# A shorter planned cost per VectorE and ScalarE operation in the scheduler of a hybrid attention and RG-LRU block

## The chip, the cores and the metric

The kernel runs on one core of one Trainium2 chip. The metric is the device time of one launch in microseconds. The version before takes 910.19 us (median of three runs, 908.47 to 910.79). Its profiled execution took 907.51 us, of which the profile's span covers 905.8 us; the remaining 1.7 us lie around the span.

TensorE is called PE in the rows, VectorE DVE, ScalarE ACT, GpSimd POOL, and the queue that issues most of the transfers SP. PEld is the loading of TensorE's stationary operand.

## The reference

One layer of a decoder block on 1024 tokens of width 1024, in float32:

```
h      = rmsnorm(x, norm_g) * (1 + scale) + shift          # scale, shift, gate from c @ w_ada
q, k, v, g_attn, xr, g_rnn, m_attn, m_rnn = split(h @ w_in)
y_attn = window_attention(rope(q), rope(k), v, sinks) * silu(g_attn)    # window 128, 16 heads, 4 kv heads
xr     = causal_depthwise_conv(xr, conv_w, conv_b)          # width 4
y_rnn  = rg_lru(xr, rg_wa, rg_wx, ...) * silu(g_rnn)        # a scan along the tokens
merged = sigmoid(m_attn) * (y_attn @ w_attn_proj) + sigmoid(m_rnn) * (y_rnn @ w_rnn_proj)
out    = rmsnorm(x + gate * (merged @ w_out), final_g)
```

The gates of the RG-LRU are products with four blocks of 256 x 256; its recurrence is `h[t] = a[t] h[t-1] + b[t]`.

## The kernel before

**Numbers.** A float32 operand is used as two float32r parts, a high one (a rounded copy, made by ScalarE) and a low one (the rest, made by VectorE); a product is the sum of high x high, high x low and low x high.

**Stages.** (1) Normalisation, transposition of x and four first column blocks. (2) The block products: the columns of `w_in`, two blocks of 128 at a time. Each such `Pair` is a 2 x 2 block product done with seven half products in Winograd's form. (3) Attention, 32 units `u` of one kv head and 128 queries each; between two units stand the last products of stage 2 and the products with `w_rnn_proj` (tile `rp`). (4) The products with `w_attn_proj`, the output projection `out`, the last norm.

**Slots.** Stage 2 and the start of stage 3 are laid out in slots. One slot holds one half product of 12 matmuls (`product`, line 711), and `SLOT` = 2.75 is what the planner thinks it takes; a gate product of the RG-LRU puts 24 matmuls (tile `pgate`, line 1027, `GATE` = 5.5) ahead of a slot's product. A pair starts every seven slots. What a pair needs at fixed slots (`at_slot`): loads of weights six to four slots ahead (tile `r`), sums of weight halves on VectorE (tile `ws`, line 733), the high parts on ScalarE two slots ahead (tile `wh`, line 106 or 108), the low parts on VectorE one slot ahead (tile `wl`, line 112 or 114), and the evacuation of PSUM banks (`keep`, `join`, the sinks).

**Background.** All else that VectorE and ScalarE do in stage 2 stands in three lists and is put between the fixed steps by `background(d)`, once per slot: `waiting[0]` (the RG-LRU after its gates: sigmoids, tanh, exp, square root, scan, `after_gates`), `waiting[1]` (the causal convolution, gate weights, the values `v` of attention) and `idle` (the gate vector and the seven combinations of `w_out`, `w_out_gate` and `w_out_blocks`; their sources are loaded into tile `wr`, their results stored to `wo_d`). Every step is a tuple of a letter, a cost on ScalarE, a cost on VectorE and a function. The planner keeps three clocks: `Load.pe`, the planned start of the slot on TensorE, and `Load.act` and `Load.dve`, when the two engines will be through with what was given to them. A group from the `waiting` lists is put when its planned end lies at most 2.8 (or 2.2) behind the slot's end, a group from `idle` when it lies at most `SLACK` behind it. No clock of the chip is read: the result is a fixed order of instructions on each engine.

The costs are written in the steps: 0.69 for a VectorE operation on 128 x 512, 0.62 for a ScalarE copy of that size, 1.22 to 1.28 for VectorE on 128 x 1024, 2.29 for the scan. The lines that spend them:

```
    def put(st_):
        Load.act = max(Load.act, Load.pe) + st_[1]
        Load.dve = max(Load.dve, Load.pe) + st_[2]
        st_[3]()
```

**Start of stage 3.** When both `waiting` lists are empty, the RG-LRU's pools are closed and `open_attn` opens those of attention, loads the second set of keys and queries (tiles `ks`, `qs`, queue SP) and the first value tiles (`vb`, `vd`, queue POOL). The first scores (tile `s_ps`, line 1338) come at a fixed slot, after 155 half products. Whatever is left in `idle` is put between the slots that follow. During attention SP further loads `ks` and `qs` of two units at a time, the gated rows `r<-ga_d`, weights `r<-w_rp`, and the RG-LRU's results (`hha`, `hla`, `yh`, `yl` from `yh_d` and `yl_d`). An instruction on SP is issued in the program's order and waits for its tile to be free.

**The tile `xc`.** The convolution writes it (`base`, then three `tap`s); it has two buffers; step `d2` of `after_gates` reads it last.

Of the kernel before, what the change touches and what calls it, by code (L numbers as in the profile page):

```python
# [55 lines left out]
def tile_hybrid_block(ctx, tc, x, pk, rows, posr, posi, c_row, w_ss, w_gate, w_main, w_v,  # L56
# [89 lines left out]
    hb = h_ctx.enter_context(tc.tile_pool(name="hb", bufs=1))  # L146
# [433 lines left out]
    W = {}  # L580
# [69 lines left out]
    class Load:  # L650

        pe = act = dve = 0.0

    def put(st_):
        Load.act = max(Load.act, Load.pe) + st_[1]
        Load.dve = max(Load.dve, Load.pe) + st_[2]
        st_[3]()

    fixed = {}
# [3 lines left out]
    def background(d):  # L663

        for n, todo in enumerate(waiting * 3):
            while todo and callable(todo[0]) and todo[0]():
                todo.pop(0)
            if not todo or callable(todo[0]):
                continue
            group, end = todo[0], Load.pe + d + (2.8 if n == 0 else 2.2 if n == 1 or "rush" in W else 0.0)  # L670
            a, v = (sum(st_[k] for st_ in group) for k in (1, 2))
            if (not a or max(Load.act, Load.pe) + a <= end) and (
                    not v or max(Load.dve, Load.pe) + v <= end):
                for st_ in todo.pop(0):
                    put(st_)
        slack = SLACK[0 if W["slot"] < 56 else 2 if all(waiting) else 1]
        for _ in range(4 if W["slot"] > 6 else 0):
            while idle and callable(idle[0]) and idle[0]():
                idle.pop(0)
            if not idle or callable(idle[0]):  # L680
                break
            a, v = (sum(st_[k] for st_ in idle[0]) for k in (1, 2))
            if (a and max(Load.act, Load.pe) + a > Load.pe + d + slack) or (
                    v and max(Load.dve, Load.pe) + v > Load.pe + d + slack):
                break
            for st_ in idle.pop(0):
                put(st_)

    def slots(d):

        t = []

        def f():
            t.append(W["slot"])
            return W["slot"] >= t[0] + d
        return f
# [187 lines left out]
    def xr_sinks(hb):  # L884
        xr = {}

        def row(ic):
            if "rn" not in W:
                open_rnn()
            if ic not in xr:  # L890
                xr[ic] = W["rn"].tile([P, S], F32, tag="xa", name="xr", bufs=2)
            return xr[ic]

        def copy(ic):
            return lambda s: [("A", 0.58, 0, lambda: A.copy(row(ic)[:, SL[0]], s()))]

        def half(ic):
            return lambda: row(ic)[:, SL[1]]

        def conv(ic):  # L900
            def add(s):
                c, t = 2 * hb + ic, {}
                x_ = xr[ic]

                def base():
                    t["xc"] = W["xcp"].tile([P, S], F32, tag="xc", name="xc")
                    A.activation(t["xc"][:], x_[:], AF.Identity,
                                 scale=pcol(PK_CW + 24, c), bias=pcol(PK_CB, c))

                def tap(k):  # L910
                    o = t["xc"][:, 3 - k:]
                    V.scalar_tensor_tensor(out=o, in0=x_[:, :S - 3 + k],
                                           scalar=pcol(PK_CW + 8 * k, c), in1=o,
                                           op0=ALU.mult, op1=ALU.add)

                def hi():
                    t["h"] = W["rn"].tile([P, S], F32R, tag="xa", name="xch", bufs=2)
                    A.copy(t["h"][:], t["xc"][:])

                def lo():  # L920
                    t["l"] = W["rn"].tile([P, S], F32R, tag="xcl", name="xcl", bufs=2)
                    V.tensor_tensor(out=t["l"][:], in0=t["xc"][:], in1=f32(t["h"][:]),
                                    op=ALU.subtract)
                    W["xc", hb, ic] = (t["h"], t["l"], t["xc"])

                taps = [("D", 0, 1.28, lambda k=k: tap(k)) for k in (2, 1, 0)]
                waiting[1].extend([[("A", 1.06, 0, base)], slots(1), *[[t_] for t_ in taps]])
                load0, split0 = gate_weights(hb, 0)
                if ic == 1:
                    waiting[1].append(load0)  # L930
                waiting[1].extend([slots(1), [("A", 1.06, 0, hi)], slots(1),
                                   [("D", 0, 1.22, lo)]])
                if ic == 1:
                    waiting[1].extend(split0 + [lambda: start_gates(hb)])
            return add

        def c12(s):
            return []

        first = copy(0)  # L940
        other = copy(1)
        return {"C11": first, "C12": (half(0), lambda s: [("N", 0, 0, lambda: conv(0)(s))]),
                "C22": (half(1), lambda s: []),
                "C21": lambda s: other(s) + [("N", 0, 0, lambda: conv(1)(s))]}
# [89 lines left out]
    def after_gates(hb, oc):  # L1034
        c, t = 2 * hb + oc, {}
        other = {"rz": "xcl", "it": "xcl", "th": "xa", "av": "xa"} if c == KC - 1 else {}

        def tl(n, tag=None, dt=F32):
            if n in other:
                t[n] = W["rn"].tile([P, S], F32, tag=other[n], name=n, bufs=2)  # L1040
            elif other:
                t[n] = t[tag] if dt == F32 else f32r(t[tag])
            else:
                t[n] = W["rn"].tile([P, S], dt, tag=tag or n, name=n)
            return t[n][:]

        def a1():
            A.activation(tl("rz"), W["g", (hb, oc)][0][:], AF.Sigmoid, bias=pcol(PK_BA, c))

        def a2():  # L1050
            A.activation(tl("it"), W["g", (hb, oc)][1][:], AF.Sigmoid, bias=pcol(PK_BX, c))

        def d1():
            V.scalar_tensor_tensor(out=t["rz"][:], in0=t["rz"][:], scalar=sp8[:, c:c + 1],
                                   in1=rbig[:], op0=ALU.mult, op1=ALU.max)

        def d2():
            V.tensor_tensor(out=t["it"][:], in0=t["it"][:], in1=W["xc", hb, oc][2][:],
                            op=ALU.mult)
            if c == KC - 1:  # L1060
                xc_ctx.close()
                W["kq", 0] = pool(at_ctx, "kq0", side="right")
                load_kq(0)

        def a3():
            A.activation(tl("th"), t["rz"][:], AF.Tanh)

        def a4():
            A.activation(tl("av"), t["rz"][:], AF.Exp, scale=-1.0)

        def a5():
            A.activation(t["rz"][:], t["av"][:], AF.Square)

        def d3():
            V.scalar_tensor_tensor(out=t["th"][:], in0=t["rz"][:], scalar=1.0, in1=t["th"][:],
                                   op0=ALU.add, op1=ALU.mult)

        def a6():
            A.activation(t["th"][:], t["th"][:], AF.Sqrt, scale=2.0 ** 20)

        def d4():
            V.scalar_tensor_tensor(out=t["it"][:], in0=t["th"][:], scalar=2.0 ** -10,
                                   in1=t["it"][:], op0=ALU.mult, op1=ALU.mult)
            dma(tl("gg", "th"), sgr_d[c])

        def d5():
            V.tensor_tensor_scan(out=t["rz"][:], data0=t["av"][:], data1=t["it"][:],
                                 initial=0.0, op0=ALU.mult, op1=ALU.add)

        def d6():  # L1090
            V.tensor_tensor(out=t["rz"][:], in0=t["rz"][:], in1=t["gg"][:], op=ALU.mult)

        def a7():
            A.copy(tl("yh", "av", F32R), t["rz"][:])  # L1094
            dma(yh_d[c], t["yh"][:], G if c == KC - 1 else nc.sync)

        def d7():
            V.tensor_tensor(out=tl("yl", "it", F32R), in0=t["rz"][:], in1=f32(t["yh"][:]),
                            op=ALU.subtract)
            dma(yl_d[c], t["yl"][:], G if c == KC - 1 else nc.sync)  # L1100

        return [[[("A", 2.4, 0, a1)]], [[("A", 1.11, 0, a2), ("D", 0, 1.28, d1)]],
                [[("A", 2.35, 0, a3)], [("D", 0, 1.22, d2)]],
                [[("A", 1.06, 0, a4), ("A", 1.06, 0, a5)]], [[("D", 0, 1.22, d3)]],
                [[("A", 2.35, 0, a6)]], [[("D", 0, 1.22, d4)], [("D", 0, 2.29, d5)]],
                [[("D", 0, 1.22, d6)]], [[("A", 1.05, 0, a7)]], [[("D", 0, 1.22, d7)]]]
# [964 lines left out]
```

## Time and profile before

| | us |
|---|---|
| median of three runs | 910.19 |
| lowest, highest run | 908.47, 910.79 |
| profiled execution | 907.51 |
| its span | 905.8 |
| TensorE busy in the span | 891.5 |
| VectorE, ScalarE, GpSimd busy | 718.2, 568.1, 185.1 |
| mean granted TensorE clock | 0.997 |

How to read it: matmuls overlap, so the busy time of TensorE says that one is always under way, not that the array is full. What matters in this profile is where TensorE stands still, and what it waits for there. A row of the timeline has start, length, engine, line, operation and tiles; the square bracket at its end is idle time of the engine ahead of it and what ended it.

### The profile page before, as it was taken

The numbers are of one execution on the slowest core, as the hardware profiler recorded it, in microseconds if no ns is written. First come the engines' busy times: TensorE is split into PE (matmuls) and PEld (weight loads), VectorE is DVE, ScalarE is ACT, GpSimd is POOL, SyncE is SP. The second block draws the span as 40 slices with busy tenths as digits, with TensorE's granted clock in tenths as the row PEclk, the third lists the DMA queues.
The fourth block names the chain that finished last, engine by engine and source line by source line (L and its number), as shares of the span: only waits on it lengthen the run. The fifth ranks groups of instructions, "written<-read, shape, count | busy, mean of one in ns | idle before, by whom it ended". The sixth has DMA issues, their size and how long they took to land.

```text
span 905.8 us, 12857 instructions
## 1 busy us (share of the span) xinstructions
PE 891.5 (98%) x4314; PEld 746.1 (82%) x4315; DVE 718.2 (79%) x1063; ACT 568.1 (63%) x1098; POOL 185.1 (20%) x331
## 2 busy tenths in 40 slices
PE   9999999999999999999999999998999999999997
PEld 6789888888888888888888888887888888888886
DVE  6988597989859875987789598898999836678855
ACT  7965564655557855786485884887888733115535
POOL 6420241200000000000000002596887720000000
PEclk9999999999999999999999999999999999999999
DMA  9829479873533353354446358999777389416504
GB/s 356 337 69 286 163 257 292 278 218 128 179 134 141 126 208 132 126 181 163 160 143 214 105 198 248 352 340 285 204 226 220 119 302 349 148 61 232 209 1 185
DMA packets 94837, 182.94 MB, mean 202 GB/s; under 512 B 15618, under 2 KB 36114, under 8 KB 94772
## 3 DMA queue, kind: packets, MB, share of 16 engines
q1 hardware_dynamic: 83200, 167.07, 53.4%
q0 software_dynamic: 11424, 14.80, 6.0%
q8 instruction: 34, 0.56, 0.3%
q14 instruction: 31, 0.25, 0.1%
q10 hardware_dynamic: 148, 0.27, 0.1%
HBM read 123.17 MB, written 59.21 MB: 201 GB/s over the span
## 4 chain that ended last, share of the span: by engine, by line
PE 91%; DVE 3%; DMA 3%; ACT 1%; POOL 1%; issue 1%; DVEq 0%; ACTq 0%; SPq 0%
PE bk L711 48%; PE rp L175 13%; PE out L1874 6%; PE pmain L175 5%; PE pgate L1027 5%; PE s_ps L1338 3%; PE bk L487 3%; PE pmain L487 2%; PE pv L1408 2%; DMA r<-w_rp 1%; DMA yl<-yl_d 1%; PE pt L1372 1%; PE pmain L1581 1%; PE pmain L1580 1%; PE pmain L1579 1%; PE bk L258 1%
## 5 line engine op out<-in xcount | busy, mean ns | idle before, releaser
L711 PE MATMUL bk<-nh,wh 128*128 128x512 f32 x368 | 143.3, 389 | 0.0
L711 PE MATMUL bk<-nl,wh 128*128 128x512 f32 x368 | 143.2, 389 | 0.0
L711 PE MATMUL bk<-nh,wl 128*128 128x512 f32 x368 | 98.4, 389 | 0.0
L106 ACT CAST wh<-r 128x512 fp32r<-128x512 f32 x107 | 65.5, 618 | 27.2 <-PE rp L175 12.8
L711 PEld LDWEIGHTS bk<-nh,wl 128*128 128x128 f32 x368 | 69.1, 188 | 14.4
L711 PEld LDWEIGHTS bk<-nh,wh 128*128 128x128 f32 x368 | 69.1, 188 | 14.2
L711 PEld LDWEIGHTS bk<-nl,wh 128*128 128x128 f32 x368 | 69.1, 188 | 14.2
L112 DVE TENSOR_TENSOR wl<-r,wh 128x512 fp32r<-128x512 f32 x91 | 62.0, 689 | 23.3 <-ACT wh L106 23.2
L63 POOL DMA_DIRECT2D yh_d<-av x1 | 0.6, 568 | 357.0 <-ACT av L1094 357.0
L711 PE MATMUL bk<-hl,wh 128*128 128x512 f32 x184 | 71.6, 389 | 0.0
L711 PE MATMUL bk<-hh,wh 128*128 128x512 f32 x184 | 71.6, 389 | 0.0
L112 DVE TENSOR_TENSOR wl<-ws,wh 128x512 fp32r<-128x512 f32 x76 | 52.0, 684 | 11.3 <-ACT wh L106 11.2
L106 ACT CAST wh<-ws 128x512 fp32r<-128x512 f32 x76 | 45.9, 614 | 7.2 <-PE bk L711 3.5
L1358 ACT ACTIVATE p<-p,small 128x129 f32<-128x129 f32 x128 | 50.0, 396 | 0.0
L711 PE MATMUL bk<-hh,wl 128*128 128x512 f32 x184 | 49.2, 389 | 0.0
L1338 PE MATMUL s_ps<-ks,qs 128*128 128x256 f32 (+1 forms) x256 | 35.8, 282 | 4.9 <-DVE yq L1427 3.0
L711 PEld LDWEIGHTS bk<-hh,wl 128*128 128x128 f32 x184 | 34.5, 188 | 7.2
L711 PEld LDWEIGHTS bk<-hh,wh 128*128 128x128 f32 x184 | 34.6, 188 | 7.1
L711 PEld LDWEIGHTS bk<-hl,wh 128*128 128x128 f32 x184 | 34.5, 188 | 7.1
L1338 PEld LDWEIGHTS s_ps<-ks,qs 128*128 128x128 f32 x256 | 32.8, 190 | 7.0 <-DVE yq L1427 3.5
L711 PE MATMUL bk<-hha,wh 128*128 128x512 f32 x92 | 35.8, 389 | 0.0
L711 PE MATMUL bk<-hla,wh 128*128 128x512 f32 x92 | 35.8, 389 | 0.0
(379 smaller groups left out, 2382.3 us busy)
## 6 DMA issues: line engine op xcount, KB each, us to landing
r<-w_main SPq DMA_DIRECT2D x100, 256.0 KB, 4.2
wada<-w_ss SPq DMA_DIRECT2D x16, 512.0 KB, 9.0
qs<-q_d SPq DMA_DIRECT2D x16, 512.0 KB, 7.5
wo_d<-wr SPq DMA_DIRECT2D x28, 256.0 KB, 2.5
wo<-wo_d SPq DMA_DIRECT2D x14, 512.0 KB, 6.2
ks<-k_d SPq DMA_DIRECT2D x12, 384.0 KB, 6.9
xt<-x SPq DMA_DIRECT2D x8, 512.0 KB, 6.8
sma_d<-c SPq DMA_DIRECT2D x16, 256.0 KB, 4.6
```

Of the source, the lines that this page charges most:

```text
L106: A.copy(dst[0][:], src)
L112: eng.tensor_tensor(out=dst[1][:], in0=src, in1=f32(dst[0][:]), op=ALU.subtract)
L175: mm = T.matmul(ps[hf], ww, xx[kc][hf], start=(kc == 0 and ww is w_h and xx is xh), stop=(kc == KC - 1 and xx is xl))
L258: T.matmul(bk[i % 2], zero[:, 0:P], zero, start=True, stop=True)
L487: T.matmul(starts[c][hf], ww[:, c0:c0 + P], xh[kc][hf], start=(kc == 0 and t_ == "h"), stop=(kc == KC - 1 and t_ == "l"))
L711: W["pe"] = T.matmul(ps, ww[:, kc * P:(kc + 1) * P], b[kc][i], start=(first and n == 0), stop=(n == 11), skip_group_check=not first)
L1027: W["pe"] = T.matmul(ps[:, SL[hf]], ww[:, c0:c0 + P], xx_[:, SL[hf]], start=(ic == 0 and i == 0), stop=(ic == 1 and i == 2))
L1338: W["pe"] = T.matmul(o, qs[:, j, qc], ks[:, kb:n % 2 + 2, b, :], start=(b == 0), stop=(b == 1))
L1358: A.activation(px[:, j, :], px[:, j, :], AF.Exp, bias=sm[:, 0, j:j + 1], accum_out=sm[:, 1, j:j + 1])
L1372: W["pe"] = T.transpose(pt[:, :, j, :], px[:, j, 0:P], ident[:])
L1408: W["pe"] = T.matmul(pv[:, cols], w, t_[:, cols], start=(i == 0), stop=(i == len(m) - 1))
L1874: T.matmul(o, a[k][x_][:, p * P:(p + 1) * P], b[k][y_][:, cols], start=(first and k == 0 and i == 0), stop=(k == 3 and i == 2), skip_group ...
```

## The change

A new function `cost` takes 0.08 from every positive cost of a step and never goes below zero. `put` and the two tests in `background` use it in place of the written numbers; `SLOT`, `GATE`, `SLACK` and the limits 2.8, 2.2 stay. Further, the group that starts a convolution (`base`) stands behind a new condition: for every block but the first it is put only once `d2` of the same half of the previous block was put (`W["used", hb, oc]`, set in `d2`).

```diff
     class Load:
 
         pe = act = dve = 0.0
 
+    def cost(st_):
+        return [max(x - 0.08, 0.0) for x in st_[1:3]]
+
     def put(st_):
-        Load.act = max(Load.act, Load.pe) + st_[1]
-        Load.dve = max(Load.dve, Load.pe) + st_[2]
+        a, v = cost(st_)
+        Load.act = max(Load.act, Load.pe) + a
+        Load.dve = max(Load.dve, Load.pe) + v
         st_[3]()
...
             group, end = todo[0], Load.pe + d + (2.8 if n == 0 else 2.2 if n == 1 or "rush" in W else 0.0)
-            a, v = (sum(st_[k] for st_ in group) for k in (1, 2))
+            a, v = (sum(cost(st_)[k] for st_ in group) for k in (0, 1))
...
-            a, v = (sum(st_[k] for st_ in idle[0]) for k in (1, 2))
+            a, v = (sum(cost(st_)[k] for st_ in idle[0]) for k in (0, 1))
...
                 taps = [("D", 0, 1.28, lambda k=k: tap(k)) for k in (2, 1, 0)]
+                waiting[1].append(lambda: hb == 0 or ("used", hb - 1, ic) in W)
                 waiting[1].extend([[("A", 1.06, 0, base)], slots(1), *[[t_] for t_ in taps]])
...
             V.tensor_tensor(out=t["it"][:], in0=t["it"][:], in1=W["xc", hb, oc][2][:],
                             op=ALU.mult)
+            W["used", hb, oc] = True
```

No instruction is added or taken away on any engine. On TensorE the 155 half products, eight gate products and one small product (line 1232) ahead of the first scores stand in the same number in a shifted order, and from the first scores on its order is the same row by row. Lines of the changed kernel are 3 to 6 higher than those of the profile.

Queue SP at the start of attention, in the kernel before: `ga_d` is the store of the gated rows, `th` and `wo_d` as above, and the rows end with the first loads of the RG-LRU's results.

```order
L63 DMA th<-sgr_d_140 128x1024
L63 DMA r<-w_main 128x512
L63 DMA ga_d_99<-c 128x2x256
L63 DMA ga_d_100<-c 128x2x256
L63 DMA wo_d_143<-wr 128x512
L63 DMA wo_d_145<-wr 128x512
L63 DMA ks<-k_d 128x768
L63 DMA qs<-q_d_93 128x1024
L63 DMA ga_d_100<-c 128x2x256
L63 DMA r<-w_rp 128x512 x2
L63 DMA wo_d_147<-wr 128x512
L63 DMA ga_d_100<-c 128x2x256
```

The same place in the changed kernel:

```order
L63 DMA th<-sgr_d_140 128x1024
L63 DMA ga_d_99<-c 128x2x256 x2
L63 DMA r<-w_main 128x512 x2
L63 DMA ga_d_99<-c 128x2x256
L63 DMA r<-w_main 128x512 x2
L63 DMA ks<-k_d 128x768
L63 DMA qs<-q_d_93 128x1024
L63 DMA ga_d_99<-c 128x2x256
L63 DMA ga_d_100<-c 128x2x256 x2
L63 DMA r<-w_rp 128x512 x2
L63 DMA ga_d_100<-c 128x2x256
```

The three stores to `wo_d` have left this stretch (they stand over a hundred rows further up), and the keys and queries `ks`, `qs` stand two stores of `ga_d` earlier.

VectorE at the end of stage 2, in the kernel before: `wl`, `ws` and `c` are the fixed work of the pairs, `it<-rz,av` (line 1098) is the RG-LRU's last operation, `wr<-wr` (line 1268) the combinations of `w_out`, and `p` and `small` the first unit of attention.

```order
L1268 TENSOR_TENSOR wr<-wr 128x512
L112 TENSOR_TENSOR wl<-r,wh 128x512
L831 SCALAR_TENSOR_TENSOR c<-c,bk_68 128x512
L771 TENSOR_TENSOR c<-u_5233,bk_71 128x512
L733 TENSOR_TENSOR ws<-ws,r 128x512
L1098 TENSOR_TENSOR it<-rz,av 128x1024
L112 TENSOR_TENSOR wl<-ws,wh 128x512
L771 TENSOR_TENSOR c<-bk_70,p_5188 128x512
L733 TENSOR_TENSOR ws<-r 128x512
L112 TENSOR_TENSOR wl<-r,wh 128x512
L831 SCALAR_TENSOR_TENSOR c<-c 128x512
L1268 TENSOR_TENSOR wr<-wr 128x512
```

The same place in the changed kernel, from the RG-LRU's last operation on:

```order
L1104 TENSOR_TENSOR it<-rz,av 128x1024
L112 TENSOR_TENSOR wl<-r,wh 128x512
L112 TENSOR_TENSOR wl<-ws,wh 128x512
L835 SCALAR_TENSOR_TENSOR c<-c,bk_69 128x512
L112 TENSOR_TENSOR wl<-ws,wh 128x512
L737 TENSOR_TENSOR ws<-r 128x512
L112 TENSOR_TENSOR wl<-r,wh 128x512
L835 SCALAR_TENSOR_TENSOR c<-c,bk_68 128x512
L775 TENSOR_TENSOR c<-u_5286,bk_71 128x512
L737 TENSOR_TENSOR ws<-ws,r 128x512
L112 TENSOR_TENSOR wl<-ws,wh 128x512
L775 TENSOR_TENSOR c<-bk_70,p_5197 128x512
```

The RG-LRU now ends several half products earlier, and the last combinations of `w_out` no longer stand between the fixed work; the last gate product stands 18 half products ahead of the first scores, where it stood 14 ahead.

VectorE in the middle of stage 2, at the second block's second scan (`rz<-av,it`, the kernel before):

```order
L1087 SCALAR_TENSOR_TENSOR rz<-av,it 128x1024
L112 TENSOR_TENSOR wl<-r,wh 128x512
L771 TENSOR_TENSOR c<-u_3901,bk_71 128x512
L733 TENSOR_TENSOR ws<-ws,r 128x512
L1091 TENSOR_TENSOR rz<-rz,gg 128x1024
L112 TENSOR_TENSOR wl<-ws,wh 128x512
```

The same scan in the changed kernel:

```order
L1093 SCALAR_TENSOR_TENSOR rz<-av,it 128x1024
L112 TENSOR_TENSOR wl<-r,wh 128x512
L1097 TENSOR_TENSOR rz<-rz,gg 128x1024
L916 SCALAR_TENSOR_TENSOR xc<-xr,pk_t,xc 128x1021
L112 TENSOR_TENSOR wl<-ws,wh 128x512 x2
```

The multiplication with `gg` and a tap of the next convolution now stand between the two low parts, where an evacuation, a weight sum and that multiplication stood.

## Prediction

> **What bounds the kernel now.** I read the head of the page first, then the shares of the chain of work that ended last.
>
> ```profile
> span 905.8 us, 12857 instructions
> PE 891.5 (98%) x4314; PEld 746.1 (82%) x4315; DVE 718.2 (79%) x1063; ACT 568.1 (63%) x1098; POOL 185.1 (20%) x331
> PE 91%; DVE 3%; DMA 3%; ACT 1%; POOL 1%; issue 1%; DVEq 0%; ACTq 0%; SPq 0%
> ```
>
> TensorE has a matmul under way in 891.5 of 905.8 us, and the chain is 91% TensorE. The change takes away no matmul. So it can win only where TensorE stands still, and lose only where it makes TensorE stand still anew. The table of windows says where that is; its columns are the window, its length, then the busy time of PE, PEld, DVE, ACT and POOL, the granted clock, the share of the DMA engines and GB/s.
>
> ```profile
> core 0: us, PE busy (x) PEld busy (x) DVE busy (x) ACT busy (x) POOL busy (x), PEclk, DMA share, GB/s
> 92.00:558.00 466.00, 466.00 (x2058) 385.84 (x2057) 377.03 (x510) 298.52 (x441) 28.59 (x52) 1.00 0.53 179
> 558.00:625.00 67.00, 61.88 (x365) 53.24 (x364) 55.99 (x97) 50.90 (x161) 41.92 (x76) 1.00 1.05 332
> 625.00:745.00 120.00, 119.95 (x696) 104.24 (x695) 100.70 (x178) 92.11 (x280) 82.73 (x146) 1.00 0.69 214
> ```
>
> The block products, where the planner works, lie in the first row: 466.00 of 466.00 us, not one stall. Nothing can be won there; every wait that appears there is a loss. The first 67 us of attention, the second row, have 67.00 − 61.88 = 5.12 us of standstill, with the DMA engines at a share of 1.05 and 332 GB/s. The third row has 0.05 us. So the most that the change can give is 5.1 us. What TensorE waits for there is in its list of waits (total, count, longest) and its timeline:
>
> ```profile
> PE s_ps L1338 <- DVE yq L1427: 3.0, 1, 3.0
> PE s_ps L1338 <- DMA qs<-q_d: 1.4, 1, 1.4
> PE s_ps L1338 <- DVE p L1365: 0.5, 1, 0.5
> PE rp L175 <- DMA yl<-yl_d: 0.2, 1, 0.2
> ```
>
> ```profile
> 574.91 1.19 PE L1338 MATMUL s_ps<-ks,qs 128*128 128x256 f32 x8 [0.45 <-DVE p L1365]
> ...
> 606.02 1.19 PE L1338 MATMUL s_ps<-ks,qs 128*128 128x256 f32 x8 [1.37 <-DMA qs<-q_d]
> ...
> 618.76 1.19 PE L1338 MATMUL s_ps<-ks,qs 128*128 128x256 f32 x8 [3.04 <-DVE yq L1427]
> ```
>
> 0.45 + 1.37 + 3.04 + 0.22 = 5.08 us, all of it. The largest is put down to VectorE, but the issue of the queries and their time to landing (least, median, most) say otherwise:
>
> ```profile
> 607.18 0.32 SPq L63 DMA_DIRECT2D qs<-q_d  x1
> ```
>
> ```profile
> DMA to landing us min/median/max: 11.4/13.1/14.2
> ```
>
> 607.18 + 11.4 = 618.6, and the scores start at 618.76: the queries end that wait too. Earlier, between 480 and 540 us, the same 512 KB took this long:
>
> ```profile
> DMA to landing us min/median/max: 3.9/3.9/3.9
> ```
>
> So 4.4 of the 5.1 us are queries that come late because some 7.5 us (11.4 − 3.9) or more of other transfers are in front of them.
>
> **The change: start of attention.** These transfers are issued as the DMA engines fill up (SP's timeline, POOL's timeline, then sizes and median time to landing of the page):
>
> ```profile
> 551.66 0.94 SPq L63 DMA_DIRECT2D wo_d<-wr  x2
> ...
> 552.71 0.36 SPq L63 DMA_DIRECT2D ks<-k_d  x1
> ...
> 553.12 1.20 SPq L63 DMA_DIRECT2D qs<-q_d  x1
> ...
> 560.17 1.37 SPq L63 DMA_DIRECT2D wo_d<-wr  x1
> ```
>
> ```profile
> 551.37 0.57 POOL L63 DMA_DIRECT2D yh_d<-av  x1 [356.97 <-ACT av L1094]
> ...
> 553.83 0.54 POOL L63 DMA_DIRECT2D yl_d<-it  x1 [1.89 <-DVE it L1098]
> ```
>
> ```profile
> qs<-q_d SPq DMA_DIRECT2D x16, 512.0 KB, 7.5
> wo_d<-wr SPq DMA_DIRECT2D x28, 256.0 KB, 2.5
> ks<-k_d SPq DMA_DIRECT2D x12, 384.0 KB, 6.9
> ```
>
> With the lower costs the combinations of `w_out` are done long before this, and the three stores to `wo_d` with them: 3 x 256 = 768 KB leave the stretch. The last gate product moves from 14 to 18 half products ahead of the first scores, and both lists of waiting work are empty three half products sooner; one is 12 matmuls at 466.00 / 2058 = 0.2264 us, so 3 x 2.72 = 8.2 us. `ks`, `qs` and the last two RG-LRU stores go that much earlier, to about 544 us, where the engines still have room (the row of 540 to 550, below, has a share of 0.72). What is taken out of the full stretch:
>
> - three stores, `ks`, `qs`: 768 + 384 + 512 = 1664 KB, 1.70 MB at 332 GB/s = **5.1 us** of transfer;
> - the two RG-LRU stores, 128 x 1024 float32 each, 1.05 MB: another 3.2 us, partly done before the stretch already.
>
> A shorter queue brings a late transfer forward only while it is never empty. The least delayed transfers of the stretch tell how much queue is always there: the RG-LRU's rows.
>
> ```profile
> L63 SPq DMA_DIRECT2D hha<-yh_d x4: 319/370/489, 563.1 to 573.6; - x4
> ```
>
> ```profile
> DMA to landing us min/median/max: 6.2/7.0/7.7
> ```
>
> 6.2 us is 3.7 us above the 2.5 us of a store of 256 KB (`wo_d` above) and 2.3 above the 3.9 of unqueued queries. So the queries of 606 and 618 us come between 2.3 and 5.1 us sooner if the queue passes its relief on, and not at all if they are bounded by something else (first rival). The two query stalls end 1.37 and 3.04 late, 4.41 together, and need 4.41 of relief to go whole; at 574.91 the wait is for `p`, VectorE's first work of a unit, and it may stay. Next in line behind a query stall is the `yl` load, 0.22. Bounds: 0 (or a little below, if earlier loads meet the last weight loads) and 5.1. I take **4.2 us**, near the upper of the two rows (3.7 + 0.5 of the further 1.05 MB), since 1.7 to 2.7 MB leave and not only what one store needs.
>
> **The change: block products.** The fixed work of VectorE and ScalarE is unmoved by rule, but more background goes ahead of it. How long an operation holds its engine, by two timelines (VectorE, then ScalarE), and when TensorE loads the low part:
>
> ```profile
> 400.89 0.69 DVE L112 TENSOR_TENSOR wl<-ws,wh 128x512 fp32r<-128x512 f32 x1
> 401.49 0.69 DVE L771 TENSOR_TENSOR c<-bk,p 128x512 f32<-128x512 f32 x1
> 402.09 0.69 DVE L733 TENSOR_TENSOR ws<-r 128x512 f32<-128x512 f32 x1
> ```
>
> ```profile
> 396.46 0.62 ACT L106 CAST wh<-ws 128x512 fp32r<-128x512 f32 x1
> 396.98 0.62 ACT L106 CAST wh<-r 128x512 fp32r<-128x512 f32 x1
> ```
>
> ```profile
> 402.02 0.87 PEld L711 LDWEIGHTS bk<-nh,wl 128*128 128x128 f32 x4
> ```
>
> A VectorE row lasts 0.69 but the next starts 0.60 later; ScalarE's 0.62 is followed after 0.52. The old cost (0.69, 0.62) was 0.09 to 0.10 above the pitch; the new one (0.61, 0.54) is 0.01 to 0.02 above it. So the lower cost is nearly the true one: the planner gives up a reserve it did not know of, and its plan still holds. The reserve that is left is read at the tightest place I found: the low part ends at 400.89 + 0.69 = 401.58, and TensorE's load of it starts at 402.02, 0.44 us later. In the busiest ten microseconds
>
> ```profile
> 110.00:120.00 10.00, 10.00 (x46) 8.29 (x45) 9.94 (x18) 6.59 (x12) 8.64 (x18) 1.00 0.63 209
> ...
> 400.00:410.00 10.00, 10.00 (x46) 8.29 (x45) 10.00 (x14) 6.56 (x11) 0.00 (x0) 1.00 0.76 260
> ...
> 540.00:550.00 10.00, 10.00 (x45) 8.28 (x45) 9.51 (x13) 6.16 (x11) 0.00 (x0) 1.00 0.72 232
> ```
>
> VectorE does 14 operations, so its backlog may grow by up to 14 x 0.08 = 1.1 us against before, 0.7 above the 0.44. That would be a wait of 0.7 us of PEld at such a place. Fifteen of the 47 stretches between 90 and 560 us have VectorE at 9.5 or more (the first of them 110, the last 540): bounds 0 and 15 x 0.7 = 10.5 us. At the tight place of before the changed order has an equal sum between the two low parts (the scan moved off, a tap moved in), so I take **0.5 us**: three quarters of one such place, near the lower end, since the pitch bears the new cost out.
>
> *A rule against the change:* the Trainium skill, page "VectorE: DVE Perf Modes", section "The DRAIN you can't avoid", says that the next operation does not start until the pipe of the last one is empty. By it the pace would be the whole 0.69 and the planner would now undercount 0.08 per operation; the starts 0.60 apart above disagree, though the page also says that a next op that is not held starts earlier. Its time is the third rival.
>
> **The change: the guard on `xc`.** It can only delay a convolution's first step, on ScalarE:
>
> ```profile
> ACT xc L907 <- DVE it L1058: 2.8, 2, 2.4
> ```
>
> ScalarE waited there twice, 2.8 us in all, in a stretch where TensorE lost nothing; now the planner waits instead, and puts other ScalarE work there. Behind the waiting instruction stood high parts (`wh`), which TensorE got in time. Cost 0, cover: the two slots by which high parts run ahead. Without that cover it would be up to 2.4 us once; bounds 0 and 2.4.
>
> **Sum.** 907.51 (905.8 of span, 1.7 around it) − 4.2 + 0.5 + 0 = 903.8. The median of the runs is 2.7 above the profiled execution: 910.2 − 3.7 = **906.5 us**. About 0.3% (2.73 us: 907.46 to 912.92) is what a measurement of this kernel can tell from no change.
>
> **Rivals.**
>
> 1. *The DMA engines are full anyway.* At a share of 1.05 over 67 us the total is set by the loads of attention itself: eight query and key loads and the RG-LRU's rows keep their places, and SP issues as soon as tiles are free. A shorter queue then makes SP issue its next load sooner, and the queue is as long at 606 us as before. For it: queries issued at 607 take 11.4 to 14.2, far more than the 6.2 to 7.7 of rows issued at 563 to 574, so the backlog grows after the moved transfers are through. Against it: tiles come free with TensorE's progress, not with the queue's, so what is issued is the same amount. Then 0.45 and half of 1.37 go, and little else: 1.1 − 0.1 = 1.0 gained, 909.2 us. Chance 0.31.
> 2. *The other side: low parts come late.* In stretches where VectorE is at 9.5 or more it has no time to work a backlog off; TensorE waits 0.7 at each, as worked out. For it: 10.00 of 10.00 busy at 400 us, with 0.44 to spare. Against it: rows last longer than their pitch, so 10.00 is not the end of what VectorE can do, and the planner still bounds the end of each group by the slot's. All fifteen: +10.5 − 4.2 = +6.3, 916.5 us. It decides from (4.2 + 2.7) / 0.7 = 10 such places up. Chance 0.10.
> 3. *The whole length of a VectorE row is its pace.* Then 15 stretches x 14 operations x 0.08 = 16.8 us of TensorE, 910.2 − 4.2 + 16.8 = 922.8 us. Starts 0.60 apart speak against it. Chance 0.02.
>
> That the change moves nothing is excluded: the order of SP and VectorE differs at the places shown.
>
> **How the numbers follow.** Forecast 0.57, rivals 0.31, 0.10, 0.02. Faster by over 0.3% is the forecast alone, 0.57; within it the first rival, 0.31; slower the other two, 0.12. The range begins where all of the 5.1 us go and the runs fall like the lowest of before (910.19 − 908.47 = 1.7): 903.5. It ends at the first rival with three late low parts, 909.2 + 2.1 = 911.3, rounded up to 911.4, and leaves out rivals two and three.
>
> **What would show it.** (a) `ks`, `qs` at about 544 instead of 552.71, no `wo_d` store behind them: the mechanism's first half. (b) Query loads near 607 landing in about 8 instead of 11.4 us, and the brackets of 3.04 and 1.37 at the scores shorter: the second half; landing times that stay mean rival one. (c) The window of the block products busy as fully as before, 466.00 of 466.00: the block term; waits of PEld or PE for `wl` at line 112, or a first score later than at 558, mean rival two, and how many there are its size. (d) No wait of ScalarE at `xc`: the guard. The prediction is wrong if the stalls of attention stay, or if the high and low parts come late more than twice.

## Result and profile after

The changed kernel takes **916.79 us** (median of four runs, 914.47 to 918.13) where the kernel before takes 909.73 beside it (908.47 to 910.79): ratio 1.0075, 95% interval 1.005 to 1.0101. Forecast were 906.5 us with a range of 903.5 to 911.4. The time went the other way, and left the range. The profiled execution took 918.13 us, 10.6 more than that of before. It is the slowest of the four, while the profiled one of before (907.51) lies below all four of its timed runs, so the profiles show 3.5 us more than the 7.1 between the medians.

The head of the page of the changed kernel, and its chain:

```profile
span 916.4 us, 12847 instructions
PE 894.6 (98%) x4315; PEld 748.0 (82%) x4315; DVE 719.4 (79%) x1063; ACT 570.7 (62%) x1100; POOL 187.8 (20%) x331
PE 83%; DMA 8%; DVE 5%; ACT 3%; issue 1%; SPq 0%; POOL 0%; DVEq 0%; ACTq 0%
```

The span is 10.6 us longer, TensorE is busy only 3.1 us longer. Transfers have gone from 3% of the chain to 8%. That is the first hint: what ends last is more often a load. The waits of TensorE (total, count, longest):

```profile
PE bk L715 <- DVE wl L114: 4.8, 1, 4.8
PE s_ps L1344 <- DMA qs<-q_d: 4.2, 1, 4.2
PE bk L715 <- DVE wl L112: 1.5, 1, 1.5
...
PE s_ps L1344 <- DVE small L1370: 0.6, 1, 0.6
```

Two waits for low parts (`wl`) are new, in the block products. The waits of attention, 4.2 + 0.6, are about the 5.1 of before. The same by windows (columns as in the prediction):

```profile
140.00:165.00 25.00, 20.20 (x80) 16.16 (x79) 17.95 (x25) 7.82 (x14) 3.07 (x5) 0.86 0.83 262
...
395.00:410.00 15.00, 13.52 (x60) 10.85 (x60) 11.98 (x16) 6.85 (x11) 0.00 (x0) 1.00 0.65 208
410.00:567.00 157.00, 157.00 (x694) 130.03 (x693) 120.96 (x157) 109.80 (x150) 6.37 (x13) 1.00 0.49 162
567.00:634.00 67.00, 62.07 (x353) 53.63 (x352) 55.95 (x96) 50.12 (x160) 40.18 (x69) 0.95 0.95 302
634.00:755.00 121.00, 120.95 (x706) 105.33 (x705) 100.83 (x178) 92.80 (x281) 83.02 (x147) 1.00 0.68 209
```

TensorE stands still for 4.80 us between 140 and 165, for 1.48 between 395 and 410, and for 4.93 in attention (5.12 before). Two of the windows also show a granted clock below 1.00, 0.86 and 0.95, which the kernel before had nowhere here.

**The first new stall.** VectorE's timeline of the changed kernel shows what held the low part back:

```profile
139.73 2.60 DVE L1215 SCALAR_TENSOR_TENSOR gate_bc<-wr,pk_t,gate_bc 128x1024 f32<-128x1024 f32 x2
...
143.45 0.68 DVE L737 TENSOR_TENSOR ws<-r 128x512 f32<-128x512 f32 x1
151.12 1.28 DVE L1215 SCALAR_TENSOR_TENSOR gate_bc<-wr,pk_t,gate_bc 128x1024 f32<-128x1024 f32 x1 [6.99 <-DMA wr<-w_gate]
152.32 0.68 DVE L114 SCALAR_TENSOR_TENSOR wl<-r,wh 128x512 fp32r<-128x512 f32 x1
```

Two steps of the gate vector (a list of `idle` work) stand in a row at 139.73. The load for the fifth step can only be issued once the third has freed its buffer. SP's timeline has it, and the view of `wr` the times to landing:

```profile
141.04 4.24 SPq L63 DMA_DIRECT2D wr<-w_gate  x2
```

```profile
DMA to landing us min/median/max: 3.2/5.8/10.0
```

It is issued at 141.04 and is the one that takes 10.0 us. In the kernel before, these loads landed faster, and the steps waited less for them:

```profile
DMA to landing us min/median/max: 4.1/5.1/6.0
```

```profile
DVE gate_bc L1209 <- DMA wr<-w_gate: 2.9, 2, 1.6
```

The fifth step is in VectorE's order one low part further on, is reached at 144.1, and VectorE stands idle for 6.99 us. The low part behind it, which TensorE needs, comes out at 153. So VectorE was not too busy: it was **idle**, waiting in order for a transfer that nobody had counted, and that took longer than before.

TensorE's timeline behind it:

```profile
153.06 2.08 PE L715 MATMUL bk<-hha,wl 128*128 128x512 f32 x4 [4.80 <-DVE wl L114]
154.93 0.63 PE L715 MATMUL bk<-nh,wh 128*128 128x512 f32 x1
155.36 0.63 PE L715 MATMUL bk<-nl,wh 128*128 128x512 f32 x1
```

The matmuls now start 0.43 us apart where the kernel before has 0.2264. The clock in the windows of the stalls and behind them, first of the changed kernel, then of the one before:

```profile
148.30:153.00 4.70, 0.00 (x0) 0.00 (x0) 1.88 (x3) 0.00 (x0) 0.00 (x0) 0.80 0.82 304
153.10:157.70 4.60, 4.60 (x11) 3.63 (x12) 4.60 (x7) 2.81 (x5) 0.00 (x0) 0.50 0.50 177
...
623.40:627.60 4.20, 0.08 (x1) 0.00 (x0) 3.56 (x8) 1.82 (x4) 3.13 (x6) 0.75 1.07 282
627.70:632.20 4.50, 4.50 (x15) 3.92 (x16) 1.67 (x4) 2.45 (x10) 1.51 (x2) 0.50 1.05 297
```

```profile
614.90:618.70 3.80, 0.82 (x6) 0.38 (x3) 3.59 (x9) 2.06 (x6) 2.19 (x5) 1.00 1.07 291
618.80:623.40 4.60, 4.38 (x25) 3.49 (x25) 2.89 (x5) 2.64 (x10) 2.67 (x4) 1.00 1.05 312
```

Behind a stall of 4.80 or 4.19 us TensorE runs some 4.6 us at a granted clock of 0.50; behind the 3.04 us of the kernel before it keeps 1.00. With some 12 matmuls at 0.43 in place of 0.2264 that is 2.5 us at the first place and about 2 at the second. The Trainium skill, page "TensorE: Matmul & The Clock Gate", section "HAM oscillation — how this bites in real kernels", puts the limit at an idle gap of about 3.4 us. These two traces lie on either side of it; a stall of 3.31 us in an experiment below cost clock too, so by these traces the limit lies between 3.04 and 3.31 us.

**The second.** VectorE, then SP, in the changed kernel:

```profile
396.29 0.67 DVE L112 TENSOR_TENSOR wl<-r,wh 128x512 fp32r<-128x512 f32 x1
399.97 1.22 DVE L1097 TENSOR_TENSOR rz<-rz,gg 128x1024 f32<-128x1024 f32 x1 [3.02 <-DMA gg<-sgr_d]
...
402.30 1.29 DVE L112 TENSOR_TENSOR wl<-ws,wh 128x512 fp32r<-128x512 f32 x2
```

```profile
381.37 11.31 SPq L63 DMA_DIRECT2D smr_d<-c  x3
...
393.71 0.42 SPq L63 DMA_DIRECT2D gg<-sgr_d  x1
```

The same kind: the multiplication with `gg` waits 3.02 us for a load that SP issued late, since a store `smr_d<-c` ahead of it waited for ScalarE. The load took 6.2 us to land, where that of the kernel before took 3.3. TensorE then waits 1.48 us for the next low part. This is one of the three places whose order the section on the change shows: the multiplication now stands one low part behind the scan, where a low part, an evacuation and a weight sum stood between.

**Attention.** The landing times of the RG-LRU's first rows (`hha`), and of the queries between 592 and 640 us:

```profile
DMA to landing us min/median/max: 3.5/4.5/5.0
```

```profile
DMA to landing us min/median/max: 12.6/13.3/14.2
```

The relief is there at `hha`, 3.5 to 5.0 in place of 6.2 to 7.7 us. At the queries nothing is left of it. Where it went is seen just ahead of `hha`, in the first 5 us behind the first scores (at 567.29 here, at 558.19 before); first the changed kernel, then the one before:

```profile
567.00:572.00 5.00, 5.00 (x31) 4.39 (x31) 2.89 (x5) 1.62 (x4) 0.00 (x0) 1.00 0.23 83
```

```profile
558.00:563.00 5.00, 5.00 (x31) 4.43 (x30) 2.99 (x5) 1.60 (x3) 1.53 (x5) 1.00 1.03 319
```

The DMA engines, full in the kernel before (1.03), have a share of 0.23 in the changed one: the queue ran empty. SP could not issue more, since a store `ga_d<-c` waited 5.8 us for VectorE; the first `hha` behind it is issued 4.96 us after the first scores in both kernels (572.25 and 563.15). So 0.77 of 5 us, 3.9 us of the DMA engines' time, went unused, most of the 5.1 us that the prediction had worked out as relief.

### The profile page after: what moved, and what is told of

The parts are those of the page before. It is cut to its first block, busy times and chain, and to the rows that moved or that the text cites. A ratio compares the mean times of both kernels' runs of the same rounds, so it can differ in the third digit from the quotient of the medians.

```text
span 916.4 us, 12847 instructions
## 1 busy us (share of the span) xinstructions
PE 894.6 (98%) x4315; PEld 748.0 (82%) x4315; DVE 719.4 (79%) x1063; ACT 570.7 (62%) x1100; POOL 187.8 (20%) x331
## 4 chain that ended last, share of the span: by engine, by line
PE 83%; DMA 8%; DVE 5%; ACT 3%; issue 1%; SPq 0%; POOL 0%; DVEq 0%; ACTq 0%
PE bk L715 41%; PE rp L175 13%; PE out L1880 6%; PE pgate L1032 5%; PE pmain L175 5%; PE s_ps L1344 3%; PE pmain L487 2%; PE bk L487 2%; PE pv L1414 2%; DMA yh<-yh_d 2%; DMA wr<-w_gate 1%; DMA qs<-q_d 1%; PE pt L1378 1%; DMA yl<-yl_d 1%; PE pmain L1587 1%
## 5 line engine op out<-in xcount | busy, mean ns | idle before, releaser
L715 PEld LDWEIGHTS bk<-nl,wh 128*128 128x128 f32 x368 | 69.7, 189 | 14.5
L715 PEld LDWEIGHTS bk<-nh,wh 128*128 128x128 f32 x368 | 69.7, 189 | 14.5
L828 ACT ACTIVATE c<-c 128x512 f32<-128x512 f32 x30 | 18.9, 631 | 36.7 <-DVE c L775 31.9
```

The lines of the kernel that those rows point to most:

```text
L715: W["pe"] = T.matmul(ps, ww[:, kc * P:(kc + 1) * P], b[kc][i], start=(first and n == 0), stop=(n == 11), skip_group_check=not first)
L828: A.activation(t["t"], s(), AF.Tanh, scale=0.5)
```

## Experiments

A name such as e1 stands for the run of that label. Theory 1: the planner clocks VectorE and ScalarE alone. With a shorter cost it puts background steps closer behind the loads they need, an engine that works in order waits there, and TensorE's low parts wait behind it. Theory 2 is the second rival of the prediction: VectorE has too little reserve. For attention: the loads of `yh` and `yl` fill the queue again, against other causes. All were timed beside the kernel before, in three batches on three chips (e1 to e4, e5 to e8, e9 and e10); its medians there were 909.13, 909.05 and 908.88.

**A gate step waits three slots after its own load (e1).** On the changed kernel:

```diff
+                t["at", k] = W["slot"]
...
         for k in range(KC):
+            idle.append(lambda k=k: W["slot"] >= t["at", k] + 3)
             idle.append(step(k))
```

> The changed kernel, with one rule more: a step of the gate vector is put only three slots after its own weight load was put. Theory 1 (the shorter cost puts background work ahead of its loads; the step at 141 us waited 7.0 us for wr<-w_gate and held a low part behind it): the stall of 4.80 us at 148 us and the slow matmuls behind it (2.5 us) go, 916.8 - 7.3 = about 909.5 us, window 140 to 165 busy 25.00 of 25.00. Theory 2 (VectorE has no reserve left, low parts come late wherever it is full): the work is only pushed into other slots, other waits for wl take its place, about 915 to 917.

Measured: 910.6 us (908.27 to 914.12), ratio to the kernel before 1.0017 (1.0006 to 1.0028). That is 1.5 above the kernel before beside it, where the changed kernel lay 7.1 above: 5.6 of the 7.1 are gone. The window of the stall, and the landing times of the same loads:

```profile
140.00:165.00 25.00, 25.00 (x112) 20.70 (x111) 19.82 (x29) 11.77 (x23) 4.64 (x8) 1.00 1.00 325
```

```profile
DMA to landing us min/median/max: 4.8/6.0/9.2
```

Stall and slow clock are gone, and nothing of their size took their place (a wait of 0.2 us for `wl` at 168 us). The costs are still 0.08 lower, and the load still takes 9.2 us; but the step that needs it stands further behind it, and TensorE does not wait for the low part after it. The rule also shifts background work behind it; the stall at 401 us was absent in this run too, though the multiplication with `gg` waited 2.4 us. So not all of the 5.6 is the one step's.

**Two slots between the scan and the multiplication with `gg` (e2).**

```diff
-                    todo.extend(step + [slots(1)])
+                    todo.extend(step + [slots(2 if i == 6 else 1)])
```

> The changed kernel, with the scan followed by two slots in place of one ahead of the multiplication with gg. Theory 1 (rz waited 3.0 us for gg<-sgr_d at 397 us, two low parts stood behind it): the stall of 1.48 us at 401 us goes, 916.8 - 1.8 = about 915. Theory 2 (VectorE too full at 400 us): the stall stays, 916.8. The stall at 148 us stays by both.

Measured: 915.71 us (914.98 to 917.9), ratio 1.0078 (1.0065 to 1.009). The window:

```profile
395.00:410.00 15.00, 15.00 (x68) 12.43 (x67) 15.00 (x18) 11.72 (x19) 0.00 (x0) 1.00 0.41 129
```

The stall went while VectorE is busy for 15.00 of 15.00 us: it keeps TensorE supplied even when completely full. A gain in time is not shown: the ratio to the kernel before was 1.0075 and is 1.0078, where 1.8 us less were expected. In the profiled executions the first scores come 1.6 us earlier after the first block product than in the changed kernel, and attention behind them takes 1.6 us longer (its two stalls are 1.41 and 3.97 us).

**Both rules (e3).**

> Both rules together. Theory 1: no stall of TensorE in the block products at all, 916.8 - 9.1 = about 907.7, no more than 1 us from the kernel before by what is left in attention. Theory 2: waits for wl at other places, 913 or more.

Measured: 909.54 us (905.89 to 910.6), ratio 0.9999 (0.9989 to 1.0009): the time of the kernel before. Its windows of the block products and, behind a stall of 3.98 us at 613.9 us, of attention:

```profile
92.00:556.00 464.00, 464.00 (x2046) 383.48 (x2045) 376.68 (x510) 297.93 (x439) 32.11 (x56) 1.00 0.55 183
```

```profile
617.60:622.20 4.60, 4.29 (x16) 3.64 (x17) 2.18 (x4) 2.64 (x10) 2.06 (x3) 0.63 1.05 298
```

464.00 of 464.00: with both orders mended, the lower costs leave TensorE without a stall in the block products. From the first block product to the first scores it is 466.6 us, against 466.05 before and 475.4 in the changed kernel. Theory 2 falls as the cause of the 9.4 us; what it may have left is the 0.5, in waits of at most 0.34 us for weight loads at 168 to 179 us, where VectorE works without a pause. In a second submission of the same kernel (e8) it took 909.74 (907.99 to 911.59), ratio 1.0012 (1.0 to 1.0024):

> The kernel of e3_both once more, on the chip of e5_filler, for the comparison of the two: 909.5.

Its profiled execution took 467.8 us for that stretch, with one wait of 0.4 us for `wl`: how much the two rules leave differs between executions.

**The loads of `yl` left out (e4).** On the changed kernel; the tile of `yh` is used in place of `yl` for the blocks 2 to 7, so the products with the low parts of these blocks are replaced by others.

```diff
-        l_ = W["yp"].tile([P, S], F32R, tag="Y", name="yl")
+        l_ = h_
         dma(h_[:], yh_d[c])
-        dma(l_[:], yl_d[c])
```

> The changed kernel without the six loads of 512 KB of yl for the blocks 2 to 7 (the tile of yh is used in their place). Queue theory (the queries at 613 and 623 us come late because the loads of yh and yl fill the queue again, whatever was moved out ahead of it): both stalls (0.58 and 4.19) and the slow matmuls behind (2.0) go, 916.8 - 6.5 = about 910.3. Rival (the scores wait for VectorE, as the list of waits had it in the kernel before, or for the tile of the queries to come free): about 916.8.

Measured: 910.68 us (909.24 to 913.94), 1.5 above the kernel before where the changed kernel lay 7.1 above, about as the queue theory had it. In its list of waits the two of the block products are left, and none of the scores:

```profile
PE bk L715 <- DVE wl L114: 4.8, 1, 4.8
...
PE bk L715 <- DVE wl L112: 1.3, 1, 1.3
```

The same edit on the kernel before (e7):

> The kernel before without the six loads of yl for the blocks 2 to 7. Queue theory: the two stalls for queries (1.37 and 3.04) and that for yl (0.22) go, 909.1 - 4.6 = about 904.5; no change of clock, since there was none. Rival (other causes): 909.

Measured: 902.02 us (901.59 to 902.45), ratio 0.9934 (0.9922 to 0.9947). The start of attention is nearly without a stall, where the kernel before had 61.88 of 67.00:

```profile
558.00:625.00 67.00, 66.18 (x394) 57.53 (x393) 60.22 (x105) 55.82 (x176) 46.16 (x83) 1.00 0.96 306
```

The gain is 7.0 us, where the stalls of the profiled execution came to only 4.6. The rest is told below.

**Half the cut (e6).** 0.04 in place of 0.08.

```diff
-        return [max(x - 0.08, 0.0) for x in st_[1:3]]
+        return [max(x - 0.04, 0.0) for x in st_[1:3]]
```

> The changed kernel with 0.04 in place of 0.08. In its order each step of the gate vector has at least two low parts between its load and itself, where the step that waited in the changed kernel had one. Theory 1 (order of load and use decides, not the size of the cost): no stall at 148 us, 909 to 911. Theory 2 (the reserve of VectorE shrinks with the cost): about half of the loss, 913.

Measured: 916.45 us (915.52 to 917.15), ratio 1.0093 (1.0079 to 1.0106): as slow as the full cut. Both expectations missed. The waits of this kernel up to 180 us:

```profile
POOL vs_d L63 <- DVE vs L1185: 35.0, 2, 22.2
...
DVE gate_bc L1215 <- DMA wr<-w_gate: 6.0, 2, 4.0
...
ACT ones_r L1225 <- POOL wr L1223: 4.2, 1, 4.2
...
PE bk L715 <- ACT wh L108: 3.3, 1, 3.3
```

The gate steps wait 6.0 us for their loads again; the longer of the two waits, 4.0 us, came with two low parts between the load and its use, so two are not enough. And a second kind has come in: ScalarE's `ones_r` waits 4.2 us for a small GpSimd write, which stands on GpSimd behind the store of `vs`, and that one waits up to 22.2 us for VectorE. GpSimd has no clock in the planner either. The loss does not grow with the size of the cut, which speaks against theory 2 again, and theory 1 holds in a wider form (any engine or transfer that isn't clocked), without a rule that says beforehand which order will hurt. The clock, in the stall of 3.31 us, behind it, and a little later:

```profile
166.90:170.20 3.30, 0.24 (x2) 0.00 (x0) 0.42 (x1) 2.91 (x6) 0.31 (x2) 1.00 0.93 220
170.40:171.70 1.30, 1.25 (x5) 1.05 (x6) 1.30 (x4) 0.52 (x2) 0.00 (x0) 0.98 0.01 3
171.70:174.60 2.90, 2.90 (x8) 2.04 (x7) 2.87 (x5) 1.13 (x3) 0.00 (x0) 0.50 0.00 0
```

The fall to 0.50 comes 1.2 us after the stall is over, with the DMA engines empty: so it is not the full queue that slows the matmuls.

**Filler matmuls in the stall of attention (e5).** On the kernel with both rules, 12 matmuls into the bank of the scores ahead of them; the scores overwrite them.

```diff
+        if u == 12:
+            for _ in range(12):
+                T.matmul(s_full[:, 0:HALF], yh[0][0][:, 0:P], yh[0][0], start=True, stop=True)
```

> The kernel of e3_both with 12 matmuls more (128x512, 2.72 us, hha into the bank of the scores, overwritten by them) ahead of the scores of unit 12, where e3 stood still for 3.98 us at 613.5 us. Clock theory (a stall of 3.7 us or more is followed by some 4.5 us at half the granted clock, one of 3.04 in the kernel before was not): the stall left is about 1.3 us, the clock in the 4.6 us behind it 1.00 instead of 0.63, and the time 1.5 to 2.0 below e3. Rival (the slow matmuls come from the full DMA engines or the loads): the clock stays low there, and the time is that of e3.

Measured: 907.83 us (906.95 to 908.23), ratio 0.999 (0.9981 to 0.9999), and 1.9 below the kernel with both rules on the same chip (909.74). Timeline and clock behind the scores:

```profile
615.90 3.02 PE L1345 MATMUL s_ps<-hha 128*128 128x512 f32 x12
619.13 1.07 PE L1349 MATMUL s_ps<-ks,qs 128*128 128x256 f32 x7 [0.21 <-DMA qs<-q_d]
```

```profile
618.70:623.30 4.60, 3.89 (x20) 2.94 (x20) 3.00 (x6) 2.64 (x10) 2.93 (x4) 1.00 1.05 293
```

The scores still come when the queries land. But TensorE does not stand still for long, and the clock stays at 1.00 with the DMA engines at 1.05. The same 12 matmuls on the kernel before (e9), and this kernel once more beside it (e10):

> The kernel before with the 12 matmuls of e5_filler ahead of the scores of unit 12, where its profiled execution stood still for 3.04 us without a loss of clock. If in most of its executions that stall is longer than in the profiled one and costs clock too (its median is 1.5 above the profiled 907.5, and e7 won 7.0 where the stalls came to 4.6): about 907.5, 1.5 below the kernel before. If not: 909, no change.

> The kernel of e5_filler once more, on the chip of e9: 907.8. If the earlier start of the loads and the stores moved away are worth something in attention, it is below e9; if the full DMA engines take it back, it is equal to e9 within 0.5.

Measured: 907.87 us (906.39 to 909.81), ratio 0.9985 (0.9975 to 0.9995), and 908.94 (907.12 to 911.36), ratio 0.9999 (0.9988 to 1.0009). The filler is worth about 1 us on the kernel before. On top of the lower cost it gave 907.83 once and 908.94 once, so nothing shows that the lower cost adds to it. In the second profile the stretch up to the first scores took 469.3 us, 3.2 more than before, and 1.0 us of waits for `wl` had come back, the longest behind this row of VectorE:

```profile
135.66 1.25 DVE L1173 TENSOR_TENSOR d<-v 64x448 f32<-64x448 f32 x2 [2.85 <-DMA v<-v_d]
```

It is the same kind once more, a background operation in front of a low part, idle for a load; the two rules do not cover it.

The granted clock of the 73 runs of the kernel before that stood beside these experiments bears on how lucky its profiled execution was:

| mean granted clock | runs | median us |
|---|---|---|
| 0.996 or more | 31 | 908.36 |
| 0.993 to 0.995 | 19 | 909.07 |
| 0.992 | 23 | 909.91 |

Of the 35 runs of the two kernels with filler 34 have 0.996 or more. The profiled execution of the kernel before, at 0.997, has the slow clock only behind its last matmul and once in the first stage:

```profile
23.47:26.88 3.41, 3.28 (x7) 2.44 (x8) 3.16 (x7) 3.38 (x6) 3.09 (x5) 0.50 1.04 400
```

That of e1 has both of these and one such stretch in attention, and has 0.994. So the 42 runs at 0.995 or less, more than half, most likely lost clock in one place more than the profiled one did. That this place is the stall of attention was not traced in those runs; that the filler there ends it speaks for it, and it also fits the 7.0 us that went with the loads of `yl`.

Not run: the shorter cost without the guard. The guard alone leaves every row of the kernel before in its place on all engines, so it was not run either. In the changed kernel ScalarE's wait at `xc`, 2.8 us in all before, is this:

```profile
ACT xc L911 <- DVE it L1063: 2.2, 1, 2.2
```

## Why the prediction was wrong

1. **What bounds the kernel**: right. TensorE, and the queries of 606 and 618 us by their loads (e4, e7), not VectorE.
2. **Block products, forecast +0.5 us**: this step failed. Measured +9.4 (475.4 us from the first block product to the first scores, 466.05 before): 4.80 of stall and 2.5 of slow clock at 148 us, 1.48 of stall and 0.3 of slow start behind it at 401, and 0.2 in small waits at 322. The step asked only how full VectorE is ("how long an operation holds its engine") and what reserve its low parts have. The stalls came from background operations that wait for something else, in front of a low part on an engine that works in order. At 401 the step even named the place, and called the sums of work between the two low parts equal; it did not ask when `gg` lands. The trace of before had the sign, unread: VectorE's `gate_bc` already waited 2.9 us for `wr<-w_gate`, in two waits of up to 1.6. The prediction's own rule, to name what is queued behind a waiting instruction, was applied to the guard only, not to the steps that moved.
3. **A shorter estimate is nearly the true pace**: right, but for half a microsecond. With the two orders mended, 464.00 of 464.00 at the full cut, and 15.00 of 15.00 with VectorE full (e2).
4. **Second rival** (slower, 916.5): near in time, wrong in cause. It wanted ten or more stretches of a full VectorE; there were two places, and VectorE was idle in both.
5. **Third rival** (the pace is the whole row, 16.8 us lost): refuted by e3, where the full cut loses 0.5. The rule of the Trainium skill, page "VectorE: DVE Perf Modes", section "The DRAIN you can't avoid", did not decide the time here.
6. **Attention, forecast −4.2 us**: this step failed too. Its first half came true: the stores to `wo_d` are gone, the keys stand at 552.77 with the first scores at 567.29, 14.5 us ahead of them where they stood 5.5 ahead (9.0 us sooner, forecast 8.2), and `hha` lands 2.7 us sooner. But the stalls went from 5.12 to 4.93 only. What failed is that the queue passes its relief on. The prediction itself says that it does so only "while it is never empty", and took the landing times of `hha` as a queue that is always there; with the relief the DMA engines stood nearly idle for 5 us ahead of `hha` (share 0.23), and the later loads filled the queue anew. The first rival (0.31) had the outcome right, and e4 and e7 show by taking the loads of `yl` out that these make the queries late. Its reason, that SP then issues its next loads sooner, is not what the rows show: `hha` is issued 4.96 us behind the first scores in both kernels.
7. **A price that no part had**: the clock behind a stall (3.31 us and more paid it, 3.04 did not). It added about 2.5 us at 148 and 2 in attention, where the two stalls of 1.37 and 3.04 had become one of 0.58 and one of 4.19, in sum 0.4 more.
8. **The guard, forecast 0**: nothing speaks against it as a cost; e3 has the guard too, and the time of the kernel before. ScalarE's wait at `xc` is not quite gone: one of 2.2 us is left, without a stall of TensorE.

The sum by what was measured: 907.5 − 0.3 (up to the first block product) + 9.4 (block products) + 1.5 (from the first scores on: −0.2 of stalls, about +2 of clock) = 918.1, against 918.13 profiled. The medians are only 7.1 apart; by the table above the profiled execution of before was one of those that lost little clock.

## What to carry to other kernels

When a planner that clocks some engines gets shorter costs, look first at the operations that also need a load or another engine: read in the new order how far each stands behind the issue of what it needs, and what stands behind it. An engine that is idle can delay more than one that is full. A transfer taken out ahead of a full stretch helps only what lands before later loads fill the queue anew; relief that the queue spends empty is lost. Follow the queue up to the transfer that is late.

## What the runs showed of the hardware

- Behind each idle gap of TensorE of 3.31 us or more (ten in these traces, 3.31 to 4.82) matmuls ran at half the granted clock; behind one of 3.04 they did not. By the traces' records of the clock each slow stretch lasted 3.4 or 6.8 us, whatever the gap: 3.4 behind one of 4.76 (e4), 6.8 behind one of 4.80 (the changed kernel). It ended 3.2 (e4) to 5.7 us (e2) behind the gap's end; at 3.31 (e6) it began only 1.2 us after that end.
- A gap is not the only thing ahead of a slow clock: in the kernel before it fell to 0.50 from 23.47 to 26.88 us, where no gap of TensorE since its first matmul was longer than 0.68 us. Why stays open.
- Twelve matmuls in the place of a gap kept the clock at 1.00 (0.63 without), and took 1.9 us off the kernel with both rules on one chip and 1.0 off the kernel before on another.
- Back to back, VectorE was busy for 15.00 of 15.00 us (e2) with rows 0.68 long started 0.60 apart, and TensorE was busy for 15.00 of 15.00.
